# v's last unit sums by DMA, gated outputs in stages, and w_out's last chunk by token halves, in a mixer and conv-FFN layer on one core

## The chip, the cores and the metric

The kernel runs on one core of a Trainium2 chip. The metric is the device time of one execution in microseconds, with the median of three runs as the time of a kernel. All numbers in the text are microseconds unless another unit stands beside them.

The engines are PE (TensorE, matmuls and transposes), DVE (VectorE), ACT (ScalarE), POOL (GpSimd) and SP (SyncE). SP issues the loads of the weights, POOL most of the other transfers. Each engine works through its instructions in the order in which they were put into its queue; a semaphore holds the first one back until what it needs is there, and everything behind it waits too.

## What is computed

One layer on 256 tokens of width 2048 in fp32: a mixer of a dilated attention branch and a gated linear attention branch (GLA), then a residual with a layer norm, then a gated FFN with a short convolution, and again residual and norm. Cut to the parts around the change:

```python
def _mixer(x, w_in, gla_gate_w, gla_gate_b, gla_norm_g, w_proj_a, w_proj_b, w_out, rel_bias):
    parts = jnp.split(x @ w_in, cuts, axis=-1)          # q, k, v of 3 groups; gq, gk, gv, gr, ...; m_a, m_b
    ...                                                  # attention: ya, GLA: o
    ya = ya.reshape(b, s, A_WIDTH).astype(x.dtype) @ w_proj_a
    o = o * lax.rsqrt(jnp.mean(o * o, axis=-1, keepdims=True) + LN_EPS) * gla_norm_g
    yb = (o.reshape(b, s, G_DV).astype(x.dtype) * jax.nn.silu(gr)) @ w_proj_b
    y = jax.nn.sigmoid(m_a) * ya + jax.nn.sigmoid(m_b) * yb
    return y @ w_out

def _conv_ffn(x, w_gate, w_up, conv_w, conv_b, w_down):
    g = x @ w_gate                                       # 2048 -> 5632
    ...                                                  # causal convolution over 3 tokens: gc
    return (jax.nn.silu(gc) * (x @ w_up)) @ w_down

mix = _mixer(x, ...)
x = _layernorm(ALPHA * x + mix, ln1_g[i], ln1_b[i])
ffn = _conv_ffn(x, ...)
x = _layernorm(ALPHA * x + ffn, ln2_g[i], ln2_b[i])
```

## The kernel before

**Weights and matmuls.** Weights come from HBM in pieces of 1 MB (128×2048 fp32). Each piece is split into a high and a low part, `whi` by ACT (L136) and `wlo` by DVE (L137), and a product is the sum of three matmuls: high × high, high × low, low × high. Activations are split likewise. The slots of `whi` (three), `wlo` (two) and of the raw pieces (`quarter`, six) go round; a piece's load waits until the split of an older piece has let go of its slot.

**Units.** The projections to v, gv, gr and m are computed in units by `seven`, a scheme with seven products in place of eight. In between it sums weight pieces: `add` is an addition on DVE (L339), `add_by_dma` an accumulating DMA that POOL issues (L342). Step p6 makes `B12 += B22` in this way, for step p7, and p2 makes `T += B21`, for p4 (whose product is called `vE` in the rows). Each is two pieces. `by_unit` asks for DVE additions in unit 0 of v alone.

**Gated outputs.** `gated_out(h)` is one of four items of the list `side`, which is worked off a bit at a time between matmuls. For each of two token halves it fetches `gr` and `o` (POOL, L114), takes the sigmoid of `gr` on ACT (`sg`, L837), multiplies it by `gr` and then by `o` on DVE (L838, L839) and has PE transpose the results (`pt`, L808), out of which ACT and DVE make the split `ob`. The items run beside the chunks `yp` of the attention branch's output projection.

**w_out and the norm.** A loop over four chunks of 512 columns computes `wo` for both token halves (`wo_t`, L260 to L262) with a piece at a time for both halves, adds it to the residual `r` (L903) and takes the statistics (L904). After the last chunk come, for each half, the aggregate (L888), the scale `rs` (ACT, L890 and L891) and `ms` (L893). Four matmuls `keep` (L908) with a matrix of ones stand in that stretch and their result is not read. Then for each of four column blocks ACT normalises `r` (L914), PE transposes it (`pt`, L921), DVE applies gain and bias by 128×256 pieces (`x1f`, L924), ACT and DVE split the result into the parts of `x` (L926, L929). The split `x` is what the FFN multiplies: three pieces first (`fg`, `fu`, `fg`, L244 and L247), then one piece at a time (`fu`, `fg`, L228 and L230), each evacuated by ACT and DVE (`pa` L252; `gbuf`, `yb` L253).

**Rows of gain and bias.** The residual of the second norm is `r` times a gain row plus a bias row. `gain` (L937, L938) does this on DVE for eight tiles, as side items; each of the sixteen rows is fetched, broadcast over the partitions, by a DMA of POOL into a slot of the pool `blk` (L879), and that pool also holds `r` and `x1f`.

**Order.** The order of the instructions on each engine is set by a scheduler when the kernel is built, by priorities and its own model of durations. A list of side work, with the slots of the pools, decides what may go ahead of what.

Of the kernel before, what the change touches and what calls it, by code (L numbers as in the profile page):

```python
# [11 lines left out]
F32 = mybir.dt.float32  # L12
F32R = mybir.dt.float32r
AF = mybir.ActivationFunctionType
# [43 lines left out]
def hybrid_layer(ctx: ExitStack, tc: tile.TileContext, wp, xt, wgl, gw, par, relb, onehot, rows, xk, out):  # L58
# [22 lines left out]
    def blk(name, dt=F32):  # L81

        n_blk[0] += 1
        return now[0].tile([P, 512], dt, tag="blk", name=f"{name}_{n_blk[0]}", bufs=now[1][0])
# [27 lines left out]
    def fetch(name, d, make=None, by=None):  # L112
        b = (make or blk)(name)
        (by or nc.gpsimd).dma_start(b, d)  # L114
        return b
# [289 lines left out]
    prm = cpool.tile([P, NPAR], F32, name="prm")  # L405
    nc.gpsimd.dma_start(prm, par)
    pc = lambda c: prm[:, c : c + 1]
    ones = cpool.tile([P, P], F32, name="ones")
    nc.gpsimd.memset(ones, 1.0)

    bvs = dpool.tile([NH, 3, 384], F32, name="bvs")
    bvd = dpool.tile([NH, 3, 32, 384], F32, name="bvd")
# [326 lines left out]

    def by_unit(name, n, sink, mark=None):  # L740
        for u in range(n):
            yield from seven(name, X, comb, AT[name, u], sink(u), by_dma=(name, u) != ("v", 0))
        yield lambda: passed.add(mark)

    tiles = of_tiles()
# [53 lines left out]
    def transposed(name, n, halves_of_tokens, gain=None):  # L799

        out = []
        r = res(name)
        for k in range(0, 4, 2):
            pt = bank("pt")
            for i in range(2):
                for t, src in enumerate(halves_of_tokens):
                    c = i * S + t * P
                    nc.tensor.transpose(pt[:, c : c + P], src[:, (k + i) * P : (k + i + 1) * P], ident)  # L808
            two = r[:, k], r[:, k + 1]
            if gain is None:  # L810
                split(*two, pt)
            else:
                for i in range(2):
                    c = slice(i * S, (i + 1) * S)
                    nc.scalar.activation(two[0][:, c], pt[:, c], AF.Copy, scale=pc(gain + k + i))
                    nc.vector.scalar_tensor_tensor(
                        two[1][:, c], pt[:, c], pc(gain + k + i), two[0][:, c].bitcast(F32), op0=ALU.mult, op1=ALU.subtract
                    )
            out.append(two)
        return out  # L820

    def by_pairs(pairs):
        def opnd(kc):
            c = slice((kc % 2) * S, (kc % 2 + 1) * S)
            return tuple(x[:, c] for x in pairs[kc // 2])
        return opnd
# [1 line left out]

    OB = []

    def gated_out(h):
        def f():
            g = []
            for t in range(2):
                x, o = fetch("gr", GR[h][t]), fetch("o", O[h][t])
                sg = blk("sg")
                nc.scalar.activation(sg, x, AF.Sigmoid)  # L837
                nc.vector.tensor_tensor(sg, sg, x, op=ALU.mult)  # L838
                nc.vector.tensor_tensor(sg, sg, o, op=ALU.mult)  # L839
                g.append(sg)  # L840
            OB.extend(transposed("ob", h, g, P_NG))
        return f

    side.extend(gated_out(h) for h in range(GH))
    last_gate = []

    def gate(br, n, t):
# [37 lines left out]
    def mean_and_scale(t):  # L885
# [7 lines left out]
        nc.vector.scalar_tensor_tensor(ms, mv[:, 0:1], -1.0, rs, op0=ALU.mult, op1=ALU.mult)  # L893
        return mv[:, 0:1], rs, ms

    for n in range(4):
        for t in range(2):
            R[t].append(blk("r"))
            nc.gpsimd.dma_start(R[t][n], xk[t * P : (t + 1) * P, n * 512 : (n + 1) * 512])
        pss = a_chunk("wo", by_pairs(YT), 16, AT["wo"] + 4 * n)  # L900
        for t in range(2):
            r = R[t][n]
            nc.vector.scalar_tensor_tensor(r, r, ALPHA, pss[t], op0=ALU.mult, op1=ALU.add)  # L903
            summed = nc.vector.bn_stats(stats[t][:, n, :], r)  # L904
    norm = [mean_and_scale(t) for t in range(2)]
    keep = bank("keep")
    for _ in range(4):
        nc.tensor.matmul(keep, ones, R[1][2], start=True, stop=True)  # L908
    X1 = [res("x1") for _ in range(4)]
    for n in range(4):  # L910
        for t in range(2):
            _, rs, ms = norm[t]
            r = R[t][n]
            nc.scalar.activation(r, r, AF.Identity, scale=rs, bias=ms)  # L914
        for k in range(0, 4, 2):
            pt = bank("pt")
            x1 = blk("x1f")
            for i in range(2):
                for t in range(2):
                    c = i * S + t * P  # L920
                    nc.tensor.transpose(pt[:, c : c + P], R[t][n][:, (k + i) * P : (k + i + 1) * P], ident)  # L921
                d = 4 * n + k + i
                c = slice(i * S, (i + 1) * S)
                nc.vector.tensor_scalar(x1[:, c], pt[:, c], pc(P_L1G + d), pc(P_L1B + d), op0=ALU.mult, op1=ALU.add)  # L924
            hi, lo = X1[n][:, k : k + 2, :S], X1[n][:, k : k + 2, S:]
            main = nc.scalar.activation(hi, x1.rearrange("p (k t) -> p k t", k=2), AF.Copy)  # L926
            if n == 2:
                held = main
            nc.vector.tensor_tensor(lo, x1.rearrange("p (k t) -> p k t", k=2), hi.bitcast(F32), op=ALU.subtract)  # L929


    ACC = R
# [211 lines left out]
```

## Time and profile before

| | us |
|---|---|
| median of 3 runs | 1894.07 |
| lowest and highest | 1893.01, 1894.31 |
| the profiled execution | 1894.48 |
| its span | 1892.8 |
| PE busy in it | 1837.2 |
| DVE busy | 1310.8 |
| ACT busy | 970.1 |
| POOL busy | 121.9 |

The span runs from the first to the last instruction of the profile; 1.7 us of the execution lie around it. PE has 9270 matmuls and transposes in it. A busy PE may still run at the lower of its two clocks, which the granted clock (PEclk) of a stretch shows: 1.00 is full speed, 0.50 half. Times in rows are counted from the start of the span.

### The profile page before, as it was taken

How to read it: one execution, taken by the hardware profiler on the slowest of the kernel's cores; microseconds unless marked ns; L12 is line 12 of the kernel's file. 1: busy time of each engine (PE TensorE's matmuls, PEld its weight loads, DVE VectorE, ACT ScalarE, POOL GpSimd, SP SyncE). 2: the span in 40 equal slices, each digit the busy share in tenths (PEclk: the TensorE clock that was granted, in tenths of full speed). 3: DMA queues.
4: the chain of work that ended last, by engine and by line, in shares of the span. 5: the costliest groups of instructions: out<-in, count | busy, mean ns of one | idle time of the engine just before them, and what ended most of it. 6: DMA issues, size and time to landing. Idle time of an engine off the chain costs nothing. (4 is left out here: it accounts for less than half of the span.)

```text
span 1892.8 us, 23057 instructions
## 1 busy us (share of the span) xinstructions
PE 1837.2 (97%) x9270; PEld 1548.0 (82%) x9270; DVE 1310.8 (69%) x1186; ACT 970.1 (51%) x963; POOL 121.9 (6%) x205
## 2 busy tenths in 40 slices
PE   7989999999999999999899998999999999999996
PEld 6778887888888888787788877888888888888885
DVE  6879978888797888764755557666546665456557
ACT  5457555555656565544643344454335554345442
POOL 0001000100101000001300001000000000000001
PEclk9999999999999999999999998999999999999998
DMA  8468986978979779794965546555555555565551
GB/s 304 157 251 275 318 307 207 326 234 263 329 230 327 231 274 331 214 325 163 333 224 195 202 160 217 179 195 183 200 189 189 189 190 193 187 243 182 196 178 45
DMA packets 80134, 432.21 MB, mean 228 GB/s; under 512 B 9857, under 2 KB 20124, under 8 KB 34076
## 3 DMA queue, kind: packets, MB, share of 16 engines
q1 hardware_dynamic: 50252, 345.06, 49.4%
q0 software_dynamic: 16240, 73.52, 15.5%
q10 hardware_dynamic: 13536, 12.16, 2.1%
q8 instruction: 72, 1.18, 0.2%
q14 instruction: 34, 0.28, 0.0%
HBM read 372.97 MB, written 21.14 MB: 208 GB/s over the span
## 5 line engine op out<-in xcount | busy, mean ns | idle before, releaser
L137 DVE TENSOR_TENSOR wlo<-quarter,whi 128x2048 fp32r<-128x2048 f32 x312 | 713.4, 2289 | 358.8 <-ACT whi L136 82.1
L136 ACT ACTIVATE whi<-quarter 128x2048 fp32r<-128x2048 f32 x312 | 597.4, 1917 | 479.1 <-PE wd_t L262 106.4
L137 DVE TENSOR_TENSOR wlo<-raw,whi 128x2048 fp32r<-128x2048 f32 (+1 forms) x75 | 165.2, 2203 | 47.3 <-ACT whi L136 23.7
L136 ACT ACTIVATE whi<-raw 128x2048 fp32r<-128x2048 f32 (+1 forms) x75 | 138.4, 1845 | 110.5 <-PE qk L228 43.2
L228 PE MATMUL qk<-x,whi 128*128 128x512 f32 x768 | 193.1, 399 | 1.5 <-ACT whi L136 1.5
L228 PE MATMUL fu<-x,whi 128*128 128x512 f32 x688 | 165.9, 394 | 5.5 <-DVE yb L253 5.5
L228 PEld LDWEIGHTS qk<-x,whi 128*128 128x128 f32 x768 | 142.0, 188 | 32.6 <-ACT whi L136 2.2
L228 PE MATMUL fg<-x,whi 128*128 128x512 f32 x672 | 160.2, 390 | 0.0
L228 PEld LDWEIGHTS fu<-x,whi 128*128 128x128 f32 x688 | 127.7, 190 | 30.6 <-issue 5.7
L228 PEld LDWEIGHTS fg<-x,whi 128*128 128x128 f32 x672 | 123.7, 188 | 24.0
L260 PE MATMUL wd_t<-whi,h 128*128 128x512 f32 x352 | 137.0, 389 | 0.0
L261 PE MATMUL wd_t<-wlo,h 128*128 128x512 f32 x352 | 137.0, 389 | 0.0
L262 PE MATMUL wd_t<-whi,h 128*128 128x512 f32 x352 | 136.9, 389 | 0.0
L230 PEld LDWEIGHTS qk<-x,wlo 128*128 128x128 f32 x768 | 98.4, 191 | 4.0 <-DVE wlo L137 0.3
L339 DVE TENSOR_TENSOR quarter<-quarter,quarter 128x2048 f32<-128x2048 f32 x44 | 100.3, 2284 | 0.4
L230 PE MATMUL qk<-x,wlo 128*128 128x256 f32 x768 | 99.7, 283 | 0.0
L230 PEld LDWEIGHTS fu<-x,wlo 128*128 128x128 f32 x688 | 88.2, 191 | 3.4
L230 PE MATMUL fu<-x,wlo 128*128 128x256 f32 x688 | 89.2, 283 | 0.0
L230 PEld LDWEIGHTS fg<-x,wlo 128*128 128x128 f32 x672 | 86.2, 191 | 3.3
L230 PE MATMUL fg<-x,wlo 128*128 128x256 f32 x672 | 87.2, 283 | 0.0
L260 PEld LDWEIGHTS wd_t<-whi,h 128*128 128x128 f32 x352 | 66.1, 188 | 13.7
L261 PEld LDWEIGHTS wd_t<-wlo,h 128*128 128x128 f32 x352 | 66.1, 188 | 13.6
(316 smaller groups left out, 2680.3 us busy)
## 6 DMA issues: line engine op xcount, KB each, us to landing
quarter<-in_wp SPq DMA_DIRECT2D x252, 1024.0 KB, 4.9
raw<-in_wp SPq DMA_DIRECT2D x71, 1024.0 KB, 6.8
quarter<-quarter POOLq DMA_DIRECT2D x36, 1024.0 KB, 12.4
row<-in_rows POOLq DMA_DIRECT2D x16, 256.0 KB, 4.6
sp<-c POOLq DMA_DIRECT2D x14, 256.0 KB, 10.9
bias<-bvd ACTq DMA_DIRECT2D x32, 96.0 KB, 4.6
v<-vs ACTq DMA_DIRECT2D x24, 128.0 KB, 2.9
m<-sp POOLq DMA_DIRECT2D x12, 256.0 KB, 4.9
```

The lines of the kernel that those rows point to most:

```text
L136: nc.scalar.activation(hi, src, AF.Copy)
L137: nc.vector.tensor_tensor(lo, src, hi.bitcast(F32), op=ALU.subtract)
L228: nc.tensor.matmul(ps, parts(kc)[0], opnd(kc), start=(kc == 0), stop=False)
L230: nc.tensor.matmul(ps[:, S:], parts(kc)[1], opnd(kc)[:, :S], start=False, stop=(kc == nk - 1))
L260: nc.tensor.matmul(ps, xh, hi, start=first, stop=False)
L261: nc.tensor.matmul(ps, xh, lo, start=False, stop=False)
L262: nc.tensor.matmul(ps, xl, hi, start=False, stop=last)
L339: tt(a, a, b, op=ALU.add)
```

## The change

There are three edits.

1. `by_unit` asks for accumulating DMAs in all units, unit 0 of v too. This concerns four sums, two in p6 and two in p2.
2. The gated outputs become six side items in place of four. Item i fetches `gr` and `o` of head i, multiplies those of head i − 1 and transposes those of head i − 2. The products are formed as `gr*o` and then `sg` times that, where they were `sg*gr` and then times `o`.
3. The last chunk of w_out takes its four pieces at once (the parts of the third and fourth in slots of `quarter`) and runs all 48 matmuls of token half 0 and then all of half 1. Half 0 is normalised by `normalised(0)` directly after its sum, so that its sixteen transposes come into the program ahead of the end of half 1; `x1f` holds one half of a block, with four TENSOR_SCALAR operations of 128×128 in place of two of 128×256 for every 512 columns. The `keep` matmuls read the identity and `r` of half 0, and the matrix of ones is gone.

```diff
     def by_unit(name, n, sink, mark=None):
         for u in range(n):
-            yield from seven(name, X, comb, AT[name, u], sink(u), by_dma=(name, u) != ("v", 0))
+            yield from seven(name, X, comb, AT[name, u], sink(u), by_dma=True)
...
-    def gated_out(h):
+    got = {}
+
+    def gated_get(h):
+        got[h] = [(fetch("gr", GR[h][t]), fetch("o", O[h][t])) for t in range(2)]
+
+    def gated_mul(h):
+        for t, (x, o) in enumerate(got[h]):
+            sg = blk("sg")
+            nc.scalar.activation(sg, x, AF.Sigmoid)
+            nc.vector.tensor_tensor(x, x, o, op=ALU.mult)
+            nc.vector.tensor_tensor(sg, sg, x, op=ALU.mult)
+            got[h][t] = sg
+
+    def gated_stage(i):
+
         def f():
-            g = []
-            for t in range(2):
-                x, o = fetch("gr", GR[h][t]), fetch("o", O[h][t])
-                sg = blk("sg")
-                nc.scalar.activation(sg, x, AF.Sigmoid)
-                nc.vector.tensor_tensor(sg, sg, x, op=ALU.mult)
-                nc.vector.tensor_tensor(sg, sg, o, op=ALU.mult)
-                g.append(sg)
-            OB.extend(transposed("ob", h, g, P_NG))
+            if i < GH:
+                gated_get(i)
+            if 0 <= i - 1 < GH:
+                gated_mul(i - 1)
+            if 0 <= i - 2 < GH:
+                OB.extend(transposed("ob", i - 2, got[i - 2], P_NG))
         return f
 
-    side.extend(gated_out(h) for h in range(GH))
+    side.extend(gated_stage(i) for i in range(GH + 2))
...
+    def normalised(t):
+
+        _, rs, ms = mean_and_scale(t)
+        for n in range(4):
+            r = R[t][n]
+            nc.scalar.activation(r, r, AF.Identity, scale=rs, bias=ms)
+            pt = bank("pt")
+            x1 = blk("x1f").rearrange("p (k t) -> p k t", k=4)
+            for k in range(4):
+                nc.tensor.transpose(pt[:, k * P : (k + 1) * P], r[:, k * P : (k + 1) * P], ident)
+            for k in range(4):
+                d = 4 * n + k
+                nc.vector.tensor_scalar(x1[:, k], pt[:, k * P : (k + 1) * P], pc(P_L1G + d), pc(P_L1B + d), op0=ALU.mult, op1=ALU.add)
+            hi, lo = X1[n][:, :, t * P : (t + 1) * P], X1[n][:, :, S + t * P : S + (t + 1) * P]
+            main = nc.scalar.activation(hi, x1, AF.Copy)
+            nc.vector.tensor_tensor(lo, x1, hi.bitcast(F32), op=ALU.subtract)
+            if n == 2:
+                held = main
+        return held
...
+        if n < 3:
+            pss = a_chunk("wo", yt, 16, AT["wo"] + 4 * n)
+            for t in range(2):
+                residual(n, t, pss[t])
+    pcs = [two_parts(load(AT["wo"] + 12 + k), spare=(k > 1)) for k in range(4)]
+    for t in range(2):
+        ps = cbank(f"wo_t{t}")
+        for k0 in range(4):
+            hi, lo = pcs[k0]
+            for k in range(4):
+                w = slice(k * 512, (k + 1) * 512)
+                kc = 4 * k0 + k
+                a_part(ps, yt(kc), hi[:, w], lo[:, w], t, kc == 0, kc == 15)
+        residual(3, t, ps)
+        if t:
+            keep = bank("keep")
+            for _ in range(4):
+                nc.tensor.matmul(keep, ident, R[0][2], start=True, stop=True)
+        held = normalised(t)
```

The removed lines of the norm did the same for blocks of both halves after the whole loop, as described above.

How the change moves instructions, at three places. Names end in a number that counts the tiles; it differs between the two kernels for the same tile.

POOL where the program leaves unit 0 of v, before (`gcs`, `gkqs` and `vs` are spills to HBM):

```order
L109 DMA gkqs_895<-gqk_808 128x512
L552 DMA vs_1_107<-s_524 128x512
L109 DMA gcs_944<-gc_942 128x512
L552 DMA vs_0_106<-c_121_984 128x512
L552 DMA vs_0_106<-u_845 128x512
```

and after:

```order
L109 DMA gkqs_893<-gqk_806 128x512
L550 DMA vs_1_105<-s_522 128x512
L109 DMA gcs_942<-gc_940 128x512
L342 DMA quarter_485<-quarter_944 128x2048
L342 DMA quarter_487<-quarter_946 128x2048
L550 DMA vs_0_104<-c_121_982 128x512
L550 DMA vs_0_104<-u_843 128x512
```

The two sums `T += B21` now stand on POOL behind the spill `gcs`; they were on DVE.

DVE from the end of w_out to the norm, before (the `r` is that of the last chunk, of half 0 and then of half 1):

```order
L903 SCALAR_TENSOR_TENSOR r_8327<-r_8327,wo_t_985_8331 128x512
L137 TENSOR_TENSOR wlo_8577<-quarter_8574,whi_8576 128x2048
L904 BN_STATS st_7935<-r_8327 128x6
L903 SCALAR_TENSOR_TENSOR r_8329<-r_8329,wo_t_986_8332 128x512
L888 BN_AGGR mv_8457<-st_7935 128x2
L904 BN_STATS st_7936<-r_8329 128x6
L893 SCALAR_TENSOR_TENSOR ms_8462<-mv_8457,rs_992_8459 128x1
L888 BN_AGGR mv_8464<-st_7936 128x2
L893 SCALAR_TENSOR_TENSOR ms_8469<-mv_8464,rs_995_8466 128x1
L924 TENSOR_SCALAR x1f_8483<-pt_8482,prm 128x256
```

and after, from the last `x1f` of half 0 to the first of half 1:

```order
L924 TENSOR_SCALAR x1f_8456<-pt_8455,prm 128x128 x4
L137 TENSOR_TENSOR wlo_8591<-quarter_8588,whi_8590 128x2048
L927 TENSOR_TENSOR x_961_7937<-x1f_8443,x_961_7937 128x4x128
L927 TENSOR_TENSOR x_962_7938<-x1f_8456,x_962_7938 128x4x128
L907 SCALAR_TENSOR_TENSOR r_8331<-r_8331,wo_t_1005_8467 128x512
L137 TENSOR_TENSOR wlo_8597<-quarter_8594,whi_8596 128x2048
L908 BN_STATS st_7934<-r_8331 128x6
L897 BN_AGGR mv_8523<-st_7934 128x2
L902 SCALAR_TENSOR_TENSOR ms_8528<-mv_8523,rs_1008_8525 128x1
L924 TENSOR_SCALAR x1f_8532<-pt_8531,prm 128x128 x4
```

All of half 0's `x1f` and its parts of `x` now stand ahead of half 1's sum, and the `wlo` of the FFN's third piece stands between that sum and its statistics, as a `wlo` did before.

DVE at the rows of gain and bias in the FFN, before:

```order
L937 TENSOR_TENSOR r_8069<-r_8069,row_9435 128x512
L938 TENSOR_TENSOR r_8069<-r_8069,row_9438 128x512
L137 TENSOR_TENSOR wlo_8714<-quarter_8711,whi_8713 128x2048
L253 TENSOR_TENSOR gbuf_6920<-fg_8586,pa_8685 128x256
L137 TENSOR_TENSOR wlo_8760<-quarter_8757,whi_8759 128x2048
L963 SCALAR_TENSOR_TENSOR gr_8688<-gbuf_6920,prm,gr_8688 128x256
L937 TENSOR_TENSOR r_8197<-r_8197,row_9535 128x512
```

and after:

```order
L963 TENSOR_TENSOR r_8199<-r_8199,row_9549 128x512
L964 TENSOR_TENSOR r_8199<-r_8199,row_9552 128x512
L137 TENSOR_TENSOR wlo_8728<-quarter_8725,whi_8727 128x2048
L253 TENSOR_TENSOR gbuf_6918<-fg_8600,pa_8699 128x256
L137 TENSOR_TENSOR wlo_8774<-quarter_8771,whi_8773 128x2048
L989 SCALAR_TENSOR_TENSOR gr_8702<-gbuf_6918,prm,gr_8702 128x256
L963 TENSOR_TENSOR r_8201<-r_8201,row_9649 128x512
```

Ten row operations stand ahead of the first `wlo` shown where eight did, the two on the fifth tile among them.

## Rows read from the trace of the kernel before

**Rows 1.** Waits of PE: for what; microseconds in total, times, longest.

```profile
PE pt L808 <- issue: 5.8, 1, 5.8
PE fu L228 <- DVE yb L253: 5.5, 1, 5.5
...
PE pt L921 <- ACT r L914: 3.8, 2, 2.0
...
PE vA L326 <- DVE wlo L137: 2.0, 3, 1.0
```

**Rows 2.** Windows: bounds, length, engines' busy time, PEclk, DMA share, GB/s.

```profile
1175.00:1179.00 4.00, 3.94 (x10) 3.15 (x11) 1.79 (x5) 1.32 (x3) 0.00 (x0) 0.53 0.61 248
...
118.00:128.40 10.40, 8.73 (x32) 6.32 (x31) 10.40 (x6) 6.80 (x5) 0.23 (x1) 0.87 0.07 25
```

**Rows 3.** Timeline of PE in the FFN: start, duration, work [idle before, releaser].

```profile
1158.27 3.82 PE L228 MATMUL fu<-x,whi 128*128 128x512 f32 x16
1161.93 2.08 PE L230 MATMUL fu<-x,wlo 128*128 128x256 f32 x16
```

**Rows 4.** Timeline of PE, a group of eight transposes.

```profile
1020.56 1.03 PE L808 MATMUL pt<-ident,m 128*128 128x128 f32 x8
```

**Rows 5.** Timeline of DVE in v's unit 0, first sum of p2.

```profile
117.32 2.27 DVE L339 TENSOR_TENSOR quarter<-quarter,quarter 128x2048 f32<-128x2048 f32 x1
```

**Rows 6.** Timeline of POOL in v's unit 0.

```profile
117.69 0.54 POOL L109 DMA_DIRECT2D gcs<-gc  x1 [4.43 <-DVE gc L635]
```

**Rows 7.** Instructions of L342: shortest, median, longest; their landing times.

```profile
L342 POOL DMA_DIRECT2D quarter<-quarter x36: 847/876/903, 148.7 to 806.6; - x36
...
DMA to landing us min/median/max: 7.6/12.4/18.8
```

**Rows 8.** Timeline of PE, start of p4's product.

```profile
132.18 2.00 PE L326 MATMUL vE<-whi,x 128*128 128x512 f32 x8
```

**Rows 9.** Page, parts 5 (busy, mean ns, idle before) and 6 (landing time).

```profile
L136 ACT ACTIVATE whi<-quarter 128x2048 fp32r<-128x2048 f32 x312 | 597.4, 1917 | 479.1 <-PE wd_t L262 106.4
...
row<-in_rows POOLq DMA_DIRECT2D x16, 256.0 KB, 4.6
```

**Rows 10.** Timelines of PE and of DVE at the first gated tile.

```profile
911.95 0.66 PE L808 MATMUL pt<-ident,sg 128*128 128x128 f32 x2 [5.76 <-issue]
...
911.16 0.69 DVE L839 TENSOR_TENSOR sg<-sg,o 128x512 f32<-128x512 f32 x1 [0.51 <-DMA o<-os]
```

**Rows 11.** Timeline of POOL, second fetch of `o`.

```profile
903.24 0.54 POOL L114 DMA_DIRECT2D o<-os  x1
```

**Rows 12.** DMA issues from 880 to 930: times, KB each, median time to landing.

```profile
o<-os POOLq DMA_DIRECT2D x8, 256.0 KB, 8.9
```

**Rows 13.** Timeline of DVE at the end of w_out.

```profile
1125.92 2.29 DVE L137 TENSOR_TENSOR wlo<-quarter,whi 128x2048 fp32r<-128x2048 f32 x1
1128.12 0.69 DVE L904 BATCH_NORM_STATS2 st<-r 128x6 f32<-128x512 f32 x1
```

**Rows 14.** Timelines of PE and of ACT around the norm.

```profile
1125.57 0.40 PE L262 MATMUL wo_t<-whi,yt 128*128 128x512 f32 x1
...
1137.84 0.80 PE L244 MATMUL fg<-x,whi 128*128 128x512 f32 x1
...
1130.36 0.81 ACT L914 ACTIVATE r<-r,ms,rs 128x512 f32<-128x512 f32 x1 [0.23 <-DVE ms L893]
```

**Rows 15.** Instructions of L924: shortest, median, longest in nanoseconds.

```profile
L924 DVE TENSOR_SCALAR x1f<-pt,prm x16: 532/538/544, 1134.0 to 1147.6; 128x256 f32<-128x256 f32 x16
```

**Rows 16.** Chain of work that ended last: start, duration, what.

```profile
1154.50 15.34 DMA row<-in_rows
```

**Rows 17.** Timeline of DVE in the FFN's first pieces.

```profile
1163.20 0.69 DVE L937 TENSOR_TENSOR r<-r,row 128x512 f32<-128x512 f32 x1 [0.94 <-DMA row<-in_rows]
...
1174.49 0.42 DVE L253 TENSOR_TENSOR yb<-fu,pa 128x256 f32<-128x256 f32 x1 [0.75 <-ACT pa L252]
```

**Rows 18.** Timeline of POOL, seven of the rows' issues.

```profile
1149.86 3.86 POOL L879 DMA_DIRECT2D row<-in_rows  x7 [1.78 <-DVE x L929]
```

More of the change, by code (lines that the diff above doesn't have):

```diff
@@ L407, in hybrid_layer @@
     pc = lambda c: prm[:, c : c + 1]
-    ones = cpool.tile([P, P], F32, name="ones")
-    nc.gpsimd.memset(ones, 1.0)
     bvs = dpool.tile([NH, 3, 384], F32, name="bvs")
@@ L894, in mean_and_scale, with residual @@
         return mv[:, 0:1], rs, ms
+    def residual(n, t, ps):
+        r = R[t][n]
+        nc.vector.scalar_tensor_tensor(r, r, ALPHA, ps, op0=ALU.mult, op1=ALU.add)
+        nc.vector.bn_stats(stats[t][:, n, :], r)
+    X1 = [res("x1") for _ in range(4)]
+    def normalised(t):
+        _, rs, ms = mean_and_scale(t)
+        for n in range(4):
+            r = R[t][n]
+            nc.scalar.activation(r, r, AF.Identity, scale=rs, bias=ms)
[12 more added lines that the diff above has]
+        return held
+    yt = by_pairs(YT)
     for n in range(4):
@@ L899, in hybrid_layer @@
             nc.gpsimd.dma_start(R[t][n], xk[t * P : (t + 1) * P, n * 512 : (n + 1) * 512])
[L900 to L929, printed above, removed]
+        if n < 3:
[17 more added lines that the diff above has]
+        held = normalised(t)
     ACC = R
```

## The prediction

> **What bounds the kernel now.** I read the shares of busy time first: TensorE (PE) works almost the whole span, so a change is worth only what it does to the gaps of PE. The waits of PE show those gaps, and four of them lie where the change cuts: 5.8 us before the gated transposes `pt` (L808), 5.5 us before a matmul `fu` of the FFN, 3.8 us before the transposes `pt` of the norm (L921), and 2.0 us at `vA` for `wlo` [rows 1]. In the windows the reader should look at the clock behind a gap: from 118 to 128.4 it is granted at 0.87, and in the four microseconds after the gap at 1175 at 0.53, the lower of the two levels (1.2 GHz, where 1.00 is 2.4) for nearly all of it [rows 2]. So a gap costs its own length and up to 4 × 0.47 = 1.9 us more. A 512-column matmul passes every (1161.93 − 1158.27) / 16 = 0.229 us [rows 3], eight 128×128 transposes take 1.03 us [rows 4]. The sum is made against the profiled execution, 1894.48 us; the median of the three runs, 1894.07, is 0.41 lower, and I take that off at the end. A measurement of this kernel can tell about 0.2%, 3.8 us, from no change.
>
> **A, the sums of v's unit 0.** Four VectorE (DVE) additions of 2.27 us go; one of them starts at 117.32, straight in the way of the `wlo` that `vA` waits for [rows 5]. With the two of `T += B21` gone, the wait of 2.0 us [rows 1] goes; the wait for `whi` just ahead is ScalarE's (ACT) and stays. The four become accumulating DMAs issued by GpSimd (POOL). The two of `B12 += B22` are issued long before they are needed and I cost them at nothing; what hides them is some tens of microseconds of other products, and without that cover `whi` of p7 would wait as below. The two of `T += B21` stand on POOL behind the spill `gcs`, 117.69 for 0.54 us [rows 6], so the first goes at 118.2, the second 0.88 us (the median issue of L342) later. Nothing else waits on POOL behind them but spills. Such sums land 7.6, 12.4 or 18.8 us after issue (shortest, median, longest of 36) [rows 7]. PE wants the first at `vE`, 132.18 [rows 8], now 2.0 us earlier, 130.2. ACT's `whi` must lie between, 1.92 us [rows 9], so a landing over 130.2 − 1.9 − 118.2 = 10.1 us is a wait: none at 7.6, 2.3 us at 12.4, 8.7 us at 18.8. The second sum is wanted 2.7 us after the first and never decides. Behind that wait stand `whi` and `wlo` of the following pieces and the load that wants the slot of `B21`. The DMA engines are busy 0.07 of the time from 118 to 128.4 [rows 2], which speaks for less than the median; I take 12.1, hence **A = −2.0 + 2.0 = 0**, with ends −2.0 and −2.0 + 8.7 = +6.7.
>
> The Trainium skill, "DMA: Bandwidth & Descriptors", section "Anatomy of one DMA — SWDGE (gpsimd) path", gives 2.0 us plus the bytes at 436 GB/s, which for 1 MB is an estimate of 4.4 us: no row here is so short, the shortest is 7.6 us [rows 7]. By it the sum would be 2.0 us lower.
>
> **B, the gated outputs in three stages.** Before, the transposes of the first gated tile start at 911.95 after 5.76 us of idle PE; DVE's product with `o` is at 911.16, having waited for the fetch `o` [rows 10]. POOL issues these fetches without a pause; the next `o` goes at 903.24 [rows 11], and with the median of 8.9 us [rows 12] it lands at 912.1. The change gives each item a stage of its own, but at the head the queue is the same, so the data come no sooner. What changes is PE's place: it does 24 matmuls of chunk 1 before the transposes instead of 10, 14 × 0.229 = 3.2 us later, arriving at 909.0 instead of 905.8. DVE now does both `gr*o` and then both `sg*gr`, 4 × 0.6 us in place of 2 × 0.6 before the first is of use: 912.1 + 0.6 + 0.6 = 913.3, and 0.4 for its way to PE gives 913.7. The idle time is 4.7 us instead of 5.8, −1.1. Against it, the load of the next weights is freed some 5 us earlier and meets the fetches: +0.6, an estimate. **B = −0.5.** Low end: `o` lands in 7.6 us, the shortest landing of a POOL transfer in these rows [rows 7], 1.3 us sooner, and the competition stays away: −2.5. High end: in the following chunk DVE has 22 to 24 short operations between two `wlo`, about 13 us by an estimate from the 0.6 to 0.7 us of such operations [rows 10], and by my count the second arrives when PE does; if it is late, by one `wlo` of 2.29 us [rows 13] and half clock behind it, +4.
>
> **C1, the norm beside w_out's second half.** Before, the last `wo` matmul is at 1125.57, a `wlo` of 2.29 us stands on DVE ahead of the last statistics (1128.12), ACT scales `r` at 1130.36, and the FFN's first `fg` is at 1137.84 [rows 13, 14]. After, half 0 ends 48 × 0.229 = 11.0 us before 1125.8, plus 0.7 for a wait on a piece split late: 1115.5. From matmul to the start of `r` it took 0.6 + (1130.36 − 1128.12) = 2.9 us, so DVE is ready for half 0's tiles at about 1118.5. Half 1 and the 16 transposes of half 0 (2.1 us, [rows 4]) end at 1128.6. DVE has until then: `wlo` 2.2, 16 x1f operations, four lo parts of 0.6, another `wlo` 2.2. A 128×128 x1f has no row; the 128×256 one takes 0.54 [rows 15], half of which is 0.27. I take 0.34, near the half with some fixed part. That makes 2.2 + 5.4 + 2.5 + 2.2 = 12.3, up to 1130.8: the last sum of half 1 starts 2.1 us late. Then the sum 0.6, a `wlo` again ahead of the statistics 2.2, statistics to `r` 2.2, `r` 0.8, four transposes 0.5, four x1f 1.4, hi and lo 0.6 each, less some 0.4 of overlap: `fg` at 1139.3, or +1.5. In exchange only 4 transposes are left behind that point instead of 14, 10 × 0.13 = −1.3, of which I count −1.0 since they filled time in which ACT and DVE worked. **C1 = +0.5.** Ends: no lateness of 2.1 on DVE, −1.6; x1f at the full 0.54, 16 × 0.2 = +3.2 more, +3.7.
>
> **C2, the gap before `fu` at 1175.** PE waited 5.5 us for DVE's `yb` at 1174.49, and the chain of waits leads back through 15.34 us of the DMA `row<-in_rows` issued last [rows 16, 17]. The rows' DMAs need slots that x1f tiles leave. After the change half 0's four x1f are free before 1131 and four rows go then, so the rest moves up, the last by some 8 us by my count. In the new order DVE has its two `gr` ahead of the `wlo` it had before them; `yb` comes about 1169.2, PE about 1170.2, no wait: **C2 = −5.5**. The half clock behind the gap, 1.9 us, is the low end, −7.4; zero (a new wait as long) the high one.
>
> **Sum.** 0 − 0.5 + 0.5 − 5.5 = −5.5: 1889.0 against the profiled time, 1888.6 as a median.
>
> **Rivals.** *The gain is only moved.* What spoke in C2 was one row; if the rows come no sooner, or `wlo` simply takes the place of `row`, PE waits there as before: 1894.48 − 0.41 = 1894.1. For it: the DMA engines are shared with weights, and a wait of 5.5 us has several sources. Against: four rows have a free slot 7 us earlier.
> *Slower: rows in front of a `wlo`.* DVE now does ten row operations ahead of the first `wlo` of the FFN's fourth piece, before eight. The ninth row was issued in the run at 1149.86 and DVE waited for it until 1163.20 [rows 17, 18]. After, it has to wait for slots that the first row operations free, near 1148. PE needs that `wlo` at 1161.93 [rows 3], the new time some 0.5 later, so the tenth row may land 10.5 us after issue, not later. The median is 4.6 us [rows 9]; at the 15.3 of the chain the `wlo` ends at 1148 + 15.3 + 0.6 + 2.3 = 1166.2, a wait of 3.8 us and half clock for 1.9: C2 = +5.7 instead of −5.5, and 1899.8.
> *The sums land late.* At 18.8 us A is +6.7, with half clock +8.6: 1897.2; at 14 it takes back half the gain of C2.
> *The sums land in under 10.1 us,* as the shortest do at 7.6 [rows 7], since the DMA engines are quiet there: A = −2.0 and 1886.6. The estimate by the Trainium skill's "DMA: Bandwidth & Descriptors" falls on this side too.
> *The stages don't do what they say:* at the head of the queue the fetches come no earlier; then B is 0, 1889.1, which changes little.
>
> **How the numbers follow.** The forecast, with the last rival in it, 0.34; the sums at the short price 0.12; together **faster 0.46**. The gain only moved, by rows or by a sum at 14 us and more, **same 0.31**. Rows in front of the `wlo` 0.12, late sums together with a part of C2 lost 0.11: **slower 0.23**. The range goes down to C2 at −7.4, A at −2.0 and B at −2.5, with C1 −0.7: 12.6 lower, 1881; up to the slower rivals, 1899. Left out are all ends at once on either side, about 2 in 10.
>
> **What would show it.** In the profile after: A right if PE no longer waits at `vA` for `wlo`, and `vE` waits for `whi` behind an L342 landing by at most 2 to 3 us; wrong if that wait is over 5. B right if the wait before L808's `pt` is still 4 to 5 us. C1 right if DVE is busy without gaps from half 0's statistics to half 1's, and the first `fg` stands about 1.5 us later than the shift of the rest makes it. C2 right if no wait of PE over 1 us is left between 1150 and 1180 and the clock there is 1.00; wrong if a wait for `wlo` behind a `row` stands there. A wait elsewhere over 3 us would make all of this wrong.

## The result, and the profile after

The changed kernel takes 1898.09 us, the median of 20 runs (1894.97 to 1901.16). The kernel before, on the same chip, takes 1893.69 (20 runs, 1889.93 to 1896.84). The ratio is 1.0024, with an interval of 1.0017 to 1.0031: **slower by 0.24%**, 4.4 us. The forecast was 1888.6, so it pointed the wrong way. The profiled execution took 1898.47, with a span of 1896.8, 4.0 longer than before.

The waits of PE come first (for what; microseconds in total, times, longest). They answer [rows 1]:

```profile
PE pt L921 <- ACT r L917: 4.0, 1, 4.0
PE pt L806 <- DVE ob L814: 3.9, 1, 3.9
PE yp_t L261 <- DVE wlo L137: 3.7, 1, 3.7
...
PE fu L228 <- DVE yb L253: 2.8, 1, 2.8
...
PE pt L806 <- issue: 2.3, 1, 2.3
```

The wait ahead of the gated transposes has fallen from 5.8 to 2.3 and the one at `fu` from 5.5 to 2.8; the `wlo` wait at `vA` is gone from its old place. Against that stand waits that were not there: 3.9 for `ob`, 3.7 for `wlo` at `yp`, and in v's unit 0 1.3 at `vE` and 2.35 at `pz`. So the time is not lost in the stage where the biggest gain was looked for. To see where it is lost I put the start of each PE instruction after beside the start of the same one before, and read how the distance grows from stage to stage:

| stretch (time before) | growth of the span, us | forecast |
|---|---|---|
| start to 108 | −1.8 | 0 |
| 108 to 150, v's unit 0 (A) | +1.9 | 0 |
| 150 to 890 | +0.4 | 0 |
| 890 to 946, gated outputs (B) | +6.5 | −0.5 |
| 946 to 1158, w_out and norm (C1) | −0.2 | +0.5 |
| 1158 to 1195, FFN's first pieces (C2) | −2.8 | −5.5 |
| 1195 to the end | 0.0 | 0 |
| sum | +4.0 | −5.5 |

The first line holds the two sums of p6, but it does not follow the change: over the kernels below it runs from −2.5 to +0.6 where nothing is altered in it, and from −2.8 to −0.7 where those sums go by DMA.

**B.** Windows of the changed kernel, then of the one before (bounds, length, busy time of PE, PEld, DVE, ACT, POOL, PEclk, DMA share, GB/s):

```profile
920.00:926.00 6.00, 2.11 (x11) 1.68 (x10) 5.77 (x11) 5.52 (x10) 1.62 (x3) 0.89 0.82 295
926.00:932.00 6.00, 6.00 (x28) 4.97 (x27) 5.64 (x12) 3.94 (x9) 2.13 (x4) 0.82 0.52 165
932.00:938.00 6.00, 2.28 (x12) 1.63 (x11) 4.45 (x7) 6.00 (x12) 2.65 (x5) 1.00 0.79 262
938.00:945.00 7.00, 7.00 (x29) 5.72 (x28) 3.69 (x3) 2.63 (x5) 0.04 (x1) 0.76 0.80 301
```

```profile
932.00:938.00 6.00, 6.00 (x32) 4.81 (x31) 5.54 (x11) 4.09 (x7) 3.21 (x6) 1.00 0.93 315
```

Before, PE was busy throughout at full clock from 920 on; one window stands for four. After, it has two holes of almost 4 us; behind the first the granted clock is 0.82 for 6 us, behind the second 0.76 for 7 us. The holes are 7.6 us long together, and the wait ahead of the first transposes is 3.2 shorter (5.8 to 2.3 + 0.3), which makes 4.4 of the 6.5. The other 2.1 is a difference and is not split here; the lower clock has a part in it. The timelines of PE, of ACT and of DVE (start, duration, work, idle before and its releaser) show what each waits for:

```profile
912.95 0.98 PE L806 MATMUL pt<-ident,sg 128*128 128x128 f32 x7 [0.26 <-DVE sg L839]
...
924.66 1.92 PE L806 MATMUL pt<-ident,sg 128*128 128x128 f32 x8 [3.89 <-DVE ob L814]
...
937.01 0.49 PE L261 MATMUL yp_t<-wlo,ya 128*128 128x512 f32 x1 [3.72 <-DVE wlo L137]
```

```profile
916.73 0.63 ACT L858 ACTIVATE m<-m 128x512 f32<-128x512 f32 x1 [5.78 <-DMA m<-sp]
917.26 1.90 ACT L136 ACTIVATE whi<-quarter 128x2048 fp32r<-128x2048 f32 x1
...
919.59 1.14 ACT L837 ACTIVATE sg<-gr 128x512 f32<-128x512 f32 x2
920.63 0.81 ACT L813 ACTIVATE ob<-pt,prm 128x256 fp32r<-128x256 f32 x2
```

```profile
920.23 1.29 DVE L838 TENSOR_TENSOR gr<-gr,o 128x512 f32<-128x512 f32 x2 [5.13 <-ACT sg L837]
...
934.67 2.28 DVE L137 TENSOR_TENSOR wlo<-quarter,whi 128x2048 fp32r<-128x2048 f32 x1
```

The first item's transposes are done by 913.9, but ACT takes them out of their banks only at 920.63. Its queue has the gate `m` ahead of that, and this gate's fetch makes ACT wait for 5.78 us, with nothing to do. Behind `m` stand `whi`, another `m` and the two sigmoids of the second item, and behind those `ob`. The second item's transposes need the banks of the first; PE reaches them after only 30 matmuls (6.8 us) and waits 3.9. DVE idles over the same time, 5.13: its next product, `gr*o`, is written over `gr`, which the sigmoid behind that `m` has still to read. It then has 24 short operations over 14.4 us (920.23 to 934.67, 1.9 of them waits) ahead of the next `wlo`, though the `whi` for it was done at 919.2, and PE waits 3.7 for this `wlo`. Before, ACT had the first `ob` and the sigmoid behind it ahead of its two `m`:

```profile
919.29 0.82 ACT L815 ACTIVATE ob<-pt,prm 128x256 fp32r<-128x256 f32 x2
920.00 0.63 ACT L837 ACTIVATE sg<-gr 128x512 f32<-128x512 f32 x1
...
921.23 1.16 ACT L849 ACTIVATE m<-m 128x512 f32<-128x512 f32 x2
```

**A.** Timelines of POOL, ACT and PE and one window of the changed kernel, to be read against [rows 2, 6, 8]:

```profile
116.42 1.81 POOL L342 DMA_DIRECT2D quarter<-quarter  x2
```

```profile
123.60 1.92 ACT L136 ACTIVATE whi<-quarter 128x2048 fp32r<-128x2048 f32 x1 [4.65 <-DMA quarter<-quarter]
130.53 1.91 ACT L136 ACTIVATE whi<-quarter 128x2048 fp32r<-128x2048 f32 x1 [4.53 <-DMA quarter<-quarter]
```

```profile
128.25 2.00 PE L326 MATMUL vE<-whi,x 128*128 128x512 f32 x8
...
132.49 1.88 PE L326 MATMUL vE<-whi,x 128*128 128x512 f32 x7 [1.33 <-ACT whi L136]
136.72 0.39 PE L625 MATMUL pz<-glp,gwp 80*128 80x256 f32 x1 [2.35 <-ACT gz L626]
...
137.18 1.07 PE L326 MATMUL vE<-wlo,x 128*128 128x512 f32 x4
```

```profile
118.00:128.40 10.40, 10.40 (x52) 8.84 (x52) 6.55 (x3) 3.35 (x3) 0.81 (x2) 0.95 1.00 198
```

The first sum is there some 7.2 us after its issue at 116.42, in time for `vE`, which starts 3.9 us earlier than before (132.18, [rows 8]), 2.1 beyond the 1.8 of the start. The second, issued 0.6 later, is there 13.5 us after its own, 6.9 after the first: the two run one after the other. PE waits 1.3 in the middle of `vE` for its `whi`, and 2.35 more at `pz`, because ACT's `gz` stands behind that late `whi` and two more. These 3.7 us take back more than the 2.1. The DMA engines, busy 0.07 of this window before, are now busy all of it.

**C.** DVE and PE around the norm, to be read against [rows 13 to 15], and the chain of work that ended last in the FFN, against [rows 16, 17]:

```profile
1126.85 2.64 DVE L924 TENSOR_SCALAR x1f<-pt,prm 128x128 f32<-128x128 f32 x8
```

```profile
1134.68 0.40 PE L262 MATMUL wo_t<-whi,yt 128*128 128x512 f32 x1
```

```profile
1137.20 0.60 DVE r L907
1137.80 2.20 DVE wlo L137
1140.00 0.62 DVE st L908
...
1174.48 1.92 PE fg L230 x16
1176.43 2.29 DVE wlo L137
1178.72 0.35 DVE yb L253
1179.20 5.50 PE fu L228 x16
```

Half 1's last matmul is at 1134.68 and DVE gets to its sum at 1137.20, with a `wlo` between that sum and the statistics. In the FFN no `row` is left in the chain. What DVE does right before `yb` is a `wlo` whose slot PE frees only at the end of the 16 `fg` matmuls.

### The profile page after: what moved, and what is told of

Its sections match the earlier page's. It is cut to its first block, busy times and chain, and to the rows that moved or that the text cites. A ratio compares the mean times of both kernels' runs of the same rounds, so it can differ in the third digit from the quotient of the medians.

```text
span 1896.8 us, 23072 instructions
## 1 busy us (share of the span) xinstructions
PE 1837.1 (97%) x9270; PEld 1550.5 (82%) x9270; DVE 1305.1 (69%) x1198; ACT 969.9 (51%) x963; POOL 125.1 (7%) x208
## 4 chain that ended last, share of the span: by engine, by line
PE 48%; DVE 2%; DMA 1%; ACT 1%; issue 0%; POOL 0%; POOLq 0%; ACTq 0%
PE fu L228 8%; PE fg L228 8%; PE fu L230 4%; PE fg L230 4%; PE wd_t L261 4%; PE wd_t L260 4%; PE wd_t L262 4%; PE pb_t L262 2%; PE pb_t L261 2%; PE pb_t L260 2%; PE wo_t L262 1%; PE wo_t L261 1%; PE wo_t L260 1%; PE fg L244 0%; DVE wlo L137 0%
## 5 line engine op out<-in xcount | busy, mean ns | idle before, releaser
L339 DVE TENSOR_TENSOR quarter<-quarter,quarter 128x2048 f32<-128x2048 f32 x40 | 91.4, 2286 | 0.4
L262 PEld LDWEIGHTS wd_t<-whi,h 128*128 128x128 f32 x352 | 66.1, 188 | 13.8
L260 PEld LDWEIGHTS wd_t<-whi,h 128*128 128x128 f32 x352 | 66.1, 188 | 13.6
```

The lines of the kernel that those rows point to most:

```text
L260: nc.tensor.matmul(ps, xh, hi, start=first, stop=False)
L262: nc.tensor.matmul(ps, xl, hi, start=False, stop=last)
L339: tt(a, a, b, op=ALU.add)
```

## The experiments

Each line of the next table is a kernel's profile against that of before, by stretches as above; "time" is the ratio of the times to those of the kernel before in the same set of runs, with its 95% interval. It is not quite the ratio of the two medians: for the halves the medians lie 3.8 us apart, and the ratio makes 5.3. The differences in microseconds below go by the ratio. The edits follow below the table.

| kernel | start | A | B | C1 | C2 | time |
|---|---|---|---|---|---|---|
| changed kernel | −1.8 | +1.9 | +6.5 | −0.2 | −2.8 | 1.0024 [1.0017, 1.0031] |
| sums only | −0.7 | +3.5 | −0.1 | | | 1.0003 [0.9994, 1.0012] |
| stages only | −0.9 | −0.1 | +6.3 | | | 1.0032 [1.0021, 1.0043] |
| halves only | −2.5 | 0.0 | +0.8 | −0.4 | −2.8 | 0.9972 [0.9960, 0.9983] |
| C with two of A's sums | −2.8 | −0.1 | +0.2 | −0.5 | −2.8 | 0.9972 [0.9962, 0.9982] |
| stages undone | −1.9 | +3.6 | +0.1 | −0.5 | −2.8 | 0.9991 [0.9981, 1.0001] |
| gates ahead | −0.7 | +2.1 | +2.4 | +0.1 | −4.4 | 1.0009 [0.9999, 1.0019] |
| one product | −2.5 | +2.1 | +1.5 | +0.2 | −4.4 | 1.0002 [0.9993, 1.0011] |
| no rows | +0.6 | 0.0 | +0.5 | −0.2 | −1.5 | 0.9985 [0.9975, 0.9994] |
| halves, first fetch | −2.3 | 0.0 | +1.6 | +0.4 | −4.4 | 0.9991 [0.9982, 1.0000] |
| `wlo` behind norm | −2.2 | 0.0 | +0.4 | −5.4 | +1.8 | 0.9977 [0.9966, 0.9987] |
| and `yb` first | −1.7 | −0.1 | −0.3 | −5.4 | −1.6 | **0.9948 [0.9934, 0.9962]** |

**One part alone.** The three kernels under the changed one are the kernel before with one of its three edits: the sums (A, this one line), the stages (B), the halves (C).

```diff
-            yield from seven(name, X, comb, AT[name, u], sink(u), by_dma=(name, u) != ("v", 0))
+            yield from seven(name, X, comb, AT[name, u], sink(u), by_dma=True)
```

> Only the sums of v's unit 0 go by DMA; gated outputs and w_out's last chunk stay as before. My theory, from the trace after: what DVE gives up near 62 to 72 us (1.8) and near 117 to 126 us (2.1) is taken back by a wait of some 4 us at vE, so the whole is within 0.5 us of the kernel before. Rival, that the sums are the cause of the slower kernel: 3 us or more slower.

> Only the gated outputs in three stages. My theory: the whole loss lies here, 6.5 us slower than the kernel before, with three waits of PE between 905 and 945 us: 2.3 at the first gated transposes, 3.9 at the second, 3.7 at a wlo. Rival, that the waits of this stretch come only together with the other two edits or are made up later: within 2 us of before.

> Only w_out's last chunk by halves of the tokens. My theory: the norm itself changes by some 0.2 us, the wait before fu falls from 5.5 to 2.8 us, and with the clock behind it the kernel is 3.0 us faster than before. Rival, that the halves give the 5.5 us forecast when the other edits are absent: 5.5 us faster. Rival, that they give nothing: within 1 us.

Measured: 1893.45, 1898.75 and 1888.79, beside 1892.63 of before. By the ratios that is +0.6 ± 1.7 for A, +6.1 ± 2.1 for B and −5.3 ± 2.2 for C. Stages alone have the 3.7 us wait for `wlo` at `yp` again, but 4.1 ahead of the first gated transposes and 1.3 for `ob`, where I expected 2.3 and 3.9. The first transposes wait longer there, since the `o` fetches land 8.6 us after their issue and not 7.2, and so PE meets the second item later. ACT's wait for `m` is nearly the same (5.62), and so is the loss. So the loss is B's own and needs neither A nor C. The three sum to +1.4 ± 3.5; the +4.5 ± 1.3 measured together is within these intervals.

**C with two of A's sums.** On top of the halves, p6's sums alone go by DMA, p2's stay on DVE.

```diff
-                (add_by_dma if by_dma else add)(a, b)
+                add_by_dma(a, b)
```

> The halves, and of unit 0's four sums only the two of p6 by DMA; the two of p2 stay on DVE, the gated outputs as before. My theory: the p6 sums alone keep their 1.8 us since PE wants them late, so this is 1.8 us faster than the halves alone and 4.8 us faster than before. Rival, that the gain of the p6 sums was an accident of the profiled run or is lost behind it: no faster than the halves alone.

Measured: 1887.8, ratio 0.9972 [0.9962, 0.9982], the same as the halves alone, where I expected 1.8 us less; its profile moves by −0.1 in A's stretch. The rival holds: the sums of p6 cost and bring nothing that can be told. What A costs comes from p2's pair.

**The stages undone in the changed kernel** (`gated_stage` replaced by the former `gated_out`, A and C kept).

> The changed kernel with the gated outputs as before: the sums by DMA and the halves stay. Theory: what the stages cost goes, about 6 us, so this is 2 us faster than the kernel before, or 5 us if the sums cost nothing as they did by themselves. Rival, that the sums lose when they come with the halves: no faster than before.

Measured: 1891.39. Taking B out turns +4.5 into −1.7 ± 1.9, so B is worth some 6 us from this side too. Together with the halves alone this kernel prices A once more: 0.9991 − 0.9972 = 0.0019, 3.6 ± 2.9 us, where A alone gave +0.6 ± 1.7. In the profiles A's stretch costs 1.9 to 3.6 in all five kernels that have both pairs. These split by the clock behind the wait at `pz`. The four matmuls `vE<-wlo` behind it take 1.07 to 1.09 where A's stretch costs 1.9 to 2.1 (the changed kernel, gates ahead, one product) and 1.91 where it costs 3.5 and 3.6 (sums only, stages undone). In "sums only":

```profile
138.29 1.91 PE L326 MATMUL vE<-wlo,x 128*128 128x512 f32 x4
```

By time A's price is not placed better than those two values and their intervals.

**Gates ahead.** The changed kernel, with the fetches of the first branch's gates `m` issued one chunk earlier.

```diff
+        if n < 3:
+            gate_get(0, n + 1)
         g = [gate(0, n, t) for t in range(2)]
```

> The changed kernel, with the gates' own fetches m of the attention branch issued one chunk ahead. Theory queue: in the changed kernel ACT stood 5.8 us for a fetch m with the evacuations ob and the sigmoids sg queued behind it; with m there earlier, ob and sg go at once, the second wait of PE (3.9 us at the transposes) goes or falls below 1 us, DVE's small operations move some 5 us up and the wait at wlo falls too: 4 to 6 us faster than the changed kernel, near the kernel before. Rival, theory DMA: the transfers of this stretch share full DMA engines, so moving fetches only moves the wait, and the time stays within 1.5 us of the changed kernel, 4.5 us slower than before.

Measured: 1894.26, ratio 1.0009, 2.8 us less than the changed kernel by the ratios; B's stretch goes from +6.5 to +2.4. The waits of PE (first lines, and further down):

```profile
PE pt L806 <- issue: 5.0, 1, 5.0
...
PE yp_t L261 <- DVE wlo L137: 1.7, 1, 1.7
```

The wait for `ob` is gone and the one for `wlo` has halved, since DVE no longer sits idle ahead of the second item's products (it starts them at 918.78, right behind a `wlo`). What came back is the wait ahead of the first transposes, 5.0. Timelines of POOL and of ACT show why:

```profile
902.67 1.60 POOL L114 DMA_DIRECT2D m<-sp  x3 [0.15 <-issue]
```

```profile
909.29 0.63 ACT L864 ACTIVATE m<-m 128x512 f32<-128x512 f32 x1 [1.87 <-DMA m<-sp]
...
913.52 1.13 ACT L837 ACTIVATE sg<-gr 128x512 f32<-128x512 f32 x2
```

Two more fetches `m` now stand on POOL ahead of the first item's, whose `gr` land at 911.8 and 913.1 where they landed at 907.6 and 910.3 in the changed kernel. The early gates and a `whi` stand on ACT ahead of the sigmoids too, which in the changed kernel were done by 910.9 and here start at 913.52. So the theory of the queue holds for the `ob` and `wlo` waits, and its rival, that moved fetches move the wait, for what came back.

**One product.** The changed kernel without the product `gr*o`; it forms only `sg*o`.

```diff
-            nc.vector.tensor_tensor(x, x, o, op=ALU.mult)
-            nc.vector.tensor_tensor(sg, sg, x, op=ALU.mult)
+            nc.vector.tensor_tensor(sg, sg, o, op=ALU.mult)
```

> The changed kernel with one of the two products left out for each gated tile (sg times o alone, without gr), so DVE has 0.6 us less for each of the 16 tiles halves and about 10 instead of 24 small operations ahead of the wlo that PE waited for. Theory queue: the 3.7 us at that wlo and the half clock behind it (about 2 us) go, the 3.9 us at the second transposes stay about 3 to 4: 5 to 6 us faster than the changed kernel. Rival, that this piece of weights itself came late (whi or its load): the wait at wlo stays, at most 1 us faster.

Measured: 1892.75, ratio 1.0002, 4.2 us less than the changed kernel by the ratios; B's stretch +1.5. The waits of PE and a row of ACT's timeline:

```profile
PE pt L806 <- DVE ob L814: 3.1, 1, 3.1
```

```profile
916.95 0.63 ACT L857 ACTIVATE m<-m 128x512 f32<-128x512 f32 x1 [5.62 <-DMA m<-sp]
```

With DVE relieved of eight operations of 0.6, the wait for `wlo` is gone and the wait for `ob` stands, with ACT still 5.62 us at `m`. The two holes thus have two causes, the gate ahead of `ob` on ACT and the pile of short operations on DVE. The gate feeds the second also: in "gates ahead" the same operations, begun earlier, made half the wait.

**No rows.** The kernel before without the row operations of the second residual.

```diff
-    side.extend(gain(n, t) for n in range(4) for t in range(2))
```

> The kernel before, with the rows of the second norm's gain and bias and their sixteen operations on DVE left out. Theory: the rows held only half of the wait of 5.5 us before fu; behind them a wlo that waits for its slot stands ahead of yb on DVE, so 2.8 us are left, as in the changed kernel. Rival, what I forecast: without rows no wait is left there, 0 to 0.5 us.

Measured: 1889.31, ratio 0.9985. PE still waits at `fu`:

```profile
PE fu L228 <- DVE yb L253: 2.8, 1, 2.8
```

It is the wait that the changed kernel has, to the tenth. My forecast that no wait is left without rows falls. Of the 5.5 us, 2.7 hung on the rows, and 2.8 on a `wlo` ahead of `yb`. That its stretch shows only −1.5 is the clock: the 16 matmuls behind the wait take 6.77 here and 5.64 in the kernel before.

**Halves, with the first item's fetches early.** On top of the halves alone, the first gated item's four fetches go ahead of the first gates' on POOL's queue.

```diff
+    early_get = [(fetch("gr", GR[0][t]), fetch("o", O[0][t])) for t in range(2)]
...
-                x, o = fetch("gr", GR[h][t]), fetch("o", O[h][t])
+                x, o = early_get[t] if h == 0 else (fetch("gr", GR[h][t]), fetch("o", O[h][t]))
```

> w_out's last chunk by halves alone, with the gated outputs as before, but the first item's four fetches issued ahead of the first gates' two. Theory: what PE waits for at the first gated transposes is the place in the queue of POOL; two fetches less ahead give 1 to 1.5 us, so the wait of 5.8 us becomes 4.5 and the kernel is 1 to 2 us faster than the halves alone. Rival: the engines are full there, all of the burst lands together, and the wait stays within 0.5 us of 5.8.

Measured: 1890.64, ratio 0.9991, and the wait has grown from 5.8 to 7.4. Timelines of PE, ACT and DVE:

```profile
910.29 0.66 PE L806 MATMUL pt<-ident,sg 128*128 128x128 f32 x2 [7.44 <-issue]
```

```profile
902.59 0.63 ACT L837 ACTIVATE sg<-gr 128x512 f32<-128x512 f32 x1
908.23 0.63 ACT L849 ACTIVATE m<-m 128x512 f32<-128x512 f32 x1 [5.02 <-DMA m<-sp]
```

```profile
903.25 0.69 DVE L838 TENSOR_TENSOR sg<-sg,gr 128x512 f32<-128x512 f32 x1 [3.72 <-ACT sg L837]
908.89 0.69 DVE L857 TENSOR_TENSOR m<-m,yp_t 128x512 f32<-128x512 f32 x1 [4.95 <-ACT m L849]
909.50 0.68 DVE L839 TENSOR_TENSOR sg<-sg,o 128x512 f32<-128x512 f32 x1
```

The sigmoid and the first product are now early, at 902.59 and 903.25. But DVE's queue has the product with `m` ahead of the one with `o`, and that `m` is now the late fetch. The order in which data land was changed and the order in which the engines ask for them was not. It is the same fault as in the changed kernel, on another engine.

**`wlo` behind the norm, and then `yb` first.** Both stand on the halves alone. The first puts the `wlo` of the FFN's second and third piece behind the low part of half 1's second block; the second, besides, puts the fourth `fg` piece's split behind the evacuation of `fu`.

```diff
+        for k, i in enumerate(idx):
+            with tc.issue_after(after.ins) if k > 0 else nullcontext():
+                ws.append(by_cols(two_parts(load(i), spare=(i == idx[-1]))))
```

```diff
+            if f == 3:
+                with tc.issue_after(up[0].ins), tc.issue_after(up[1].ins):
+                    ps = b16("fg", x1op, at)
```

> w_out's last chunk by halves alone, and the wlo of the FFN's second and third piece put behind the norm's work on DVE. Theory: in the changed kernel two wlo of 2.2 us each stand on DVE ahead of half 1's statistics, the first making its sum 2.2 us late, the second between sum and statistics; without them the wait of 4.0 us before half 1's transposes falls below 1 us and the kernel is about 4 us faster than the halves alone, 8 to 9 us faster than before. Rival: the pieces' lo parts are then late for the FFN, or the wait turns up at fg or fu: no faster than the halves alone.

> The same, and in the FFN the split of the piece for the fourth fg is put behind the evacuation yb of the second fu, on ACT and on DVE. Theory: the 2.8 us that are left before fu come from that split, which waits for its slot ahead of yb; with yb first the wait falls below 1 us, and with the half clock behind it the kernel is 2 to 4 us faster than the one with the two wlo moved. Rival: the late split makes the next fg wait instead: no faster.

Measured: 1889.5, ratio 0.9977, no better than the halves alone; and 1884.62, ratio 0.9948 [0.9934, 0.9962], 9.8 us below the kernel before by the ratio (8.6 between the medians). Timeline of PE, the first kernel and then the second:

```profile
1129.93 1.36 PE L914 MATMUL pt<-ident,r 128*128 128x128 f32 x8 [0.68 <-ACT r L910]
...
1169.49 5.40 PE L229 MATMUL fu<-x,whi 128*128 128x512 f32 x16 [7.53 <-DVE yb L257]
```

```profile
1164.59 6.74 PE L229 MATMUL fu<-x,whi 128*128 128x512 f32 x16 [2.82 <-DVE yb L258]
```

Without the `wlo` pieces ahead of the sum and of the statistics, the norm's wait falls from 4.0 to 0.7 and its stretch from −0.4 to −5.4. With that edit alone the gain is given back 40 us on, where a `wlo` and rows stand ahead of `yb` and the wait is 7.5. Ordering that one split behind `yb` keeps the gain. The wait at `fu` is 2.8 then, not below 1 as I expected: two row operations stand on DVE right ahead of that `yb` (1162.79 to 1164.12). The last kernel beats both of the kernels compared here.

## Why the prediction failed

**B is the step that failed,** with −0.5 forecast and +6.5 by the profile (+6.1 ± 2.1 alone). Its first half held: the same fetches at the head of the queue, an idle time ahead of the first transposes shorter by more than forecast (2.3 + 0.3, where I said 4.7), because the `o` fetches landed 7.2 us after issue and not 8.9. The failure is in "what changes is PE's place". I followed the first item to PE and stopped there. By staging, the second item's sigmoid and the first item's evacuation came to stand behind a gate whose fetch makes ACT wait 5.8 us, and PE met two full banks. No term or rival had that: the rival on the stages said they would do nothing, at a price of 0. The `wlo` that came late I had, with its place and its cause, as the high end of +4. The price was near (3.7 and a lower clock behind it); the choice of "it arrives when PE does" was not, since DVE's short operations began 5.1 us late for the same gate. "A wait elsewhere over 3 us would make all of this wrong" is what the profile then showed.

**A: the value was too low, for a reason I had excluded.** The first sum came in 7.2 us, under the limit of 10.1, so by my working A should have gained 2.0, and `vE` did start 2.1 earlier. I wrote that the second sum "never decides"; it decides, because the two ran one after the other and the second lands 6.9 after the first, not 0.9. The quiet DMA engines, which I took to speak for short landings, were filled by the sums themselves (0.07 to 1.00 of the window). The cost of 1.9 to 3.6 in the profiles lies inside the ends of −2.0 to +6.7, but by a wait that the ends were not made for.

The estimate of 4.4 us by the Trainium skill, "DMA: Bandwidth & Descriptors", section "Anatomy of one DMA — SWDGE (gpsimd) path", differs from both landings here, 7.2 for the first and 13.5 for the second. The measurement decides. The rival on the page's side had its condition met by the first sum, and lost its gain to the second.

**C1 held.** DVE was to get to half 1's sum 2.1 late; the last matmul starts at 1134.68 and ends 0.40 later, the sum starts at 1137.20, 2.1 behind it. A 128×128 `x1f` in a row takes 2.64 / 8 = 0.33, where 0.34 was taken. The first `fg` was to stand 1.5 later than the rest makes it: it starts at 1146.06, and 1146.06 − 1137.84 is 8.2, of which 7.0 is the shift of the rest, so 1.2. The whole stretch came out at −0.2 instead of +0.5, inside the ends.

**C2 had the mechanism and half the size:** −2.8 for −5.5. The rows did move up and none is waited for. But a wait has a second cause behind its first. I had looked for what DVE does ahead of that `wlo` and not at the `wlo` itself, which stands ahead of `yb` and needs the slot that PE holds until its last `fg` matmul. "No rows" shows the same 2.8 with no row at all. "Rows in front of a `wlo`" did not happen: no wait for a row is in the changed kernel's chain there.

**The sum.** From −5.5 forecast, B adds 7.0, C2 2.7, A 1.9, C1 takes 0.7, the stretch from 150 to 890 adds 0.4, and the start takes 1.8: +4.0, the span's difference. That the time lies inside the range is luck: its upper end, 1899, came from late rows and a late first sum, and B, the largest part of the loss, came from neither.

Three slips in the working change nothing here. In B the idle time before was taken as 5.76 but PE's arrival as the start of its last matmul, 905.8; by one measure the saving is 1.5 and not 1.1. The 7.6 us of [rows 7] for `o` is a landing of a 1 MB sum, not of a 256 KB fetch. And the tenth row could land 11.5 us after issue without a wait (15.3 − 3.8), not 10.5.

What stays open: why A costs +0.6 by time alone and 3.5 in its profile. The eleven executions of "sums only" fall into two groups, six from 1890.9 to 1893.5 and five from 1895.9 to 1898.1, and the profile is of the longest, so it is a poor price for A; there is none of the lower group. Nor is it settled what sets the first 108 us, which differ by over 3 us from profile to profile.

## What to carry to other kernels

When work is put in stages, follow each engine's queue past the first item: ask which of its instructions now stand behind one that waits for a DMA, and who needs the buffers that those would free. Data that land early help only if the engines ask for them in that order. And before a wait is booked as gained, name the next instruction in that queue and the slot it needs; here that left half the wait standing, while two small changes of order, of splits behind work that PE waits for, brought another 4.5 ± 3.4 us (0.9972 to 0.9948).

## What the runs showed of the hardware

Two accumulating DMAs of 1 MB within SBUF, issued 0.6 us apart, were there 7.2 and 13.5 us after their issue, with the DMA engines busy throughout at 198 GB/s. Both stand in POOL's queue. These landings fit one transfer at a time, in this kernel and in "sums only" alike (ACT's two `whi` 6.9 apart in both).

The lower clock does not always follow the same gap. In the changed kernel and in "gates ahead" PE waits the same 2.81 us before `fu`, yet the 16 matmuls behind it take 5.50 in the one and 3.91 in the other. Windows of the first kernel, then of the second, each within these matmuls (1179.20 to 1184.70 and 1176.48 to 1180.39):

```profile
1182.00:1184.00 2.00, 2.00 (x6) 1.57 (x5) 0.00 (x0) 0.00 (x0) 0.00 (x0) 0.50 0.51 209
```

```profile
1178.00:1180.00 2.00, 2.00 (x11) 1.64 (x9) 0.61 (x2) 0.42 (x1) 0.00 (x0) 1.00 1.00 422
```

The granted clock is 0.50 (1.2 GHz) in the one and 1.00 (2.4 GHz) in the other. That is the 1.6 us between −2.8 and −4.4 in the column C2 above. Halves alone and "halves, first fetch", which have the same code there, lie on its two sides (5.51 and 3.92), so it is no part of what an edit there is worth.
